# Up projection of a hybrid block: which engine makes the token operands, where the raw rows lie, and weights that stay across the change of tokens

## The chip, the cores and the metric

One core of one Trainium2 chip runs the whole kernel. The metric is device time in microseconds (us), median of several runs of the same program. TensorE does the matrix products (PE, with its weight loads as PEld), VectorE (DVE) and GpSimd (POOL) do elementwise work, ScalarE (ACT) casts, copies and activations, and the queue of SyncE (SP) issues nearly all transfers.

## The reference, cut to what matters

```python
h = h + concat([y_s5, y_rwkv]) @ w_out          # output projection
hn = rms_norm(h, norm_ffn_g)
h = h + square(relu(hn @ w_up)) @ w_down        # up projection, down projection
return rms_norm(h, norm_final_g)
# 2048 tokens, D_MODEL 1024, D_FF 4096, all float32
```

The change touches only the up projection, `square(relu(hn @ w_up))`.

## The kernel before, in words

**The product.** Every float32 operand is split in a high and a low part: ScalarE casts the high part (`hi`, tiles whose names end in h), and an elementwise subtraction makes the low part (`lo`, names in l). A product is then three matmuls (hh, hl, lh) for each block of 128 of the contraction (`product`, L1322). On top of that the up projection is done as a Strassen-like scheme with seven products in place of eight, in the order `ORDER = (1, 5, 6, 2, 7, 3, 4)` (L1283). The weights of a product are sums of quarter blocks a, b, c, d (`left_sums`, L1286, four additions), and so are the tokens (`right_sums`, L1305, four additions for each half, so eight for a set).

**The loops.** `mlp_up` (L1359) has two halves of the tokens (`hb` 0 and 1, 1024 tokens each). For each half it walks over 16 pairs of output blocks (`f` = 0, 2, ... 30), seven products each, twelve matmuls of 128x128x512 for a product. The token operands `x[n]` (seven of them, 128x1024 twice for `hi` and `lo`) stay for a whole half; the weights of a pair are made anew for each `f` and each half, by the generator `ws()`, which `Ahead` keeps up to `UA` = 4 operands in front.

**The making of token operands.** `xs(hb)` loads six raw rows `xraw` of 4 KB per partition from `x2_dram` (quarters a, b, d, two tiles each) into a ring `raw` of seven buffers (L1372), which it shares with the raw weights `wraw` (two tiles for a pair). The quarter c goes into two buffers of the ring `xrow2` (three buffers, L1398). For each n, `xs` takes the sums (L1309 to L1318), casts (L1402) and subtracts (L1403). In half 0 the sums are on VectorE and four of the fourteen subtractions (n = 2 and 3) on GpSimd; in half 1 the sums are on GpSimd and all subtractions on VectorE. The operands 1, 5, 6 have tiles of their own (`mux`); 2, 7, 3, 4 lie in the tiles of the output projection's weights `wo`, so they can't be written before that projection has ended.

**The change of tokens.** While pair f = 30 of half 0 runs, `xs(1)` writes each operand anew as soon as its last product of half 0 has been issued (L1517 to L1520).

**What comes out.** Four of the seven results of a pair are split again (`operands`, L1464: sum, cast L1468, subtraction L1469) and both parts are written to `hs_d` (L1471). Their tiles come from the ring `ys` (sixteen buffers of 2 KB), which also holds the weights' `hi` and `lo`.

**Before and after.** The output projection (`out_proj`) ends in two calls of `proj` that `mlp_up` makes itself (`last[0]`, `last[1]`), between the first operands. Its pools of the GLU (`oe0`, `oe`) and of the group norm (`opl`) are given back before `mlp_up` opens its own, so the new tiles lie at their addresses: `mux` (48 KB) first, then `mur`, the raw rows (28 KB). `mlp_down` follows.

**Order.** The order of instructions on each queue is not written by hand: a planner takes, at each moment of its own timeline, what is ready and has a buffer, and of several the one that stands first in the program. A load with nothing to wait for can thus be issued far ahead of its place.

Of the kernel before, what the change touches and what calls it, by code (L numbers as in the profile page):

```python
# [7 lines left out]
F32 = mybir.dt.float32  # L8
F32R = mybir.dt.float32r
I32 = mybir.dt.int32  # L10
AF = mybir.ActivationFunctionType
ALU = mybir.AluOpType
AX = mybir.AxisListType
PSUM = bass.MemoryType.PSUM
DRAM = bass.MemoryType.DRAM
P = 128
# [6 lines left out]
def pool_of(tc, **k):  # L23
    return tc.tile_pool(reuse_waits="tile", **k)
# [339 lines left out]
BT = 512  # L364
# [712 lines left out]
UA, DW, DH = 4, 2, 3  # L1077
# [208 lines left out]
def left_sums(eng, q, new):  # L1286

    (a, b), (c, d) = q
    yield a
    s = new()  # L1290
    eng.tensor_tensor(out=s, in0=c, in1=d, op=ALU.add)
    yield s
    s2 = new()
    eng.tensor_tensor(out=s2, in0=s, in1=a, op=ALU.subtract)  # L1294
    yield s2
    yield b
    eng.tensor_tensor(out=c, in0=a, in1=c, op=ALU.subtract)
    yield c
    s = new()
    eng.tensor_tensor(out=s, in0=b, in1=s2, op=ALU.subtract)  # L1300
    yield s
    yield d


def right_sums(eng, q):  # L1305

    (a, b), (_, d) = q
    yield a
    eng.tensor_tensor(out=a, in0=b, in1=a, op=ALU.subtract)  # L1309
    yield a  # L1310
    eng.tensor_tensor(out=a, in0=d, in1=a, op=ALU.subtract)  # L1311
    yield a
    c = q[1][0]
    yield c
    eng.tensor_tensor(out=b, in0=d, in1=b, op=ALU.subtract)  # L1315
    yield b
    yield d
    eng.tensor_tensor(out=a, in0=c, in1=a, op=ALU.subtract)  # L1318
    yield a
# [39 lines left out]
def mlp_up(K, opened, h_dram, x2_dram, norm_g, w_up, hs_dram, hr_dram):  # L1359
# [3 lines left out]
    v, act, g = nc.vector, nc.scalar, nc.gpsimd  # L1363
    H = KT // 2
    from contextlib import ExitStack
    with ExitStack() as st:
        pool_ = lambda **k: st.enter_context(pool_of(tc, **k))
        oc, oy, ops, last = opened
        xp, rp, cp, hp, psp = pool_(name="mux", bufs=1), pool_(name="mur", bufs=1), pool_(name="muc", bufs=1), pool_(name="muh", bufs=1), pool_(name="mups", bufs=2, space=PSUM)
        gain = column(K, cp, norm_g[0], KT, "gain2")  # L1370
        wu = w_up[0].rearrange("(k p) m -> p k m", p=P)
        raw = lambda shape, name: rp.tile(shape, F32, tag="raw", bufs=7, name=name)  # L1372
# [10 lines left out]
        def xs(hb):  # L1383

            qs = [[[None, None], [None, None]] for _ in range(0, H, 2)]

            def load(i, j, t, o):
                qs[i][j][t] = o
                nc.sync.dma_start(out=o, in_=x2_dram[hb * 2 + t, :, j * H + 2 * i:j * H + 2 * i + 2])

            for j, t in ((0, 0), (0, 1), (1, 1)):
                for i in range(H // 2):
                    load(i, j, t, raw([P, 2, BT], "xraw"))
            parts = [right_sums((v, g)[hb], q) for q in qs]
            for n in ORDER:
                if n == 2:
                    for i in range(H // 2):
                        load(i, 1, 0, oy.tile([P, 2, BT], F32, tag="xrow2", bufs=3, name="xraw"))  # L1398
                hi, lo = xtile(n)
                for i, part in enumerate(parts):  # L1400
                    r = next(part)
                    act.copy(out=hi[i], in_=r)  # L1402
                    (g if hb == 0 and n in (2, 3) else v).tensor_tensor(out=lo[i], in0=r, in1=hi[i].bitcast(F32), op=ALU.subtract)  # L1403
                hi, lo = ([t[i // 2][:, i % 2] for i in range(H)] for t in (hi, lo))
                x[n] = hi, lo
                yield

        def ws():

            def load(f):  # L1410
                r = [raw([P, H, 2 * P], "wraw") for _ in range(2)]
                for j in range(2):
                    nc.sync.dma_start(out=r[j], in_=wu[:, j * H:j * H + H, f * P:f * P + 2 * P])
                return [[r[j][:, :, i * P:i * P + P] for j in range(2)] for i in range(2)]

            nxt = load(0)
            for n in range(32):
                q = nxt
                for i, o in enumerate(left_sums(g, q, lambda: cp.tile([P, H, P], F32, tag="s", bufs=2, name="ws"))):
                    if i == 0 and n < 31:  # L1420
                        nxt = load(2 * (n + 1) % 32)
                    hi, lo = (oy.tile([P, H, P], F32R, tag="ys", bufs=16, name="w" + s) for s in "hl")
                    act.copy(out=hi, in_=o)  # L1423
                    v.tensor_tensor(out=lo, in0=o, in1=hi.bitcast(F32), op=ALU.subtract)  # L1424
                    yield tuple([t[:, k] for k in range(H)] for t in (hi, lo))

        def last_norm(b):
# [9 lines left out]
            for k in range(KT):  # L1437
# [9 lines left out]
                if k % 2:  # L1447
                    yield

        w, nx = Ahead(ws(), UA), xs(0)  # L1450
        next(nx)
        last[0]()
        w.fill()
        next(nx)
        next(nx)
        last[1]()
        ct = 0

        def hid(name):
            nonlocal ct  # L1460
# [3 lines left out]
        def operands(hb, fp, q):  # L1464

            def split_(n, o):
                hi, lo = (oy.tile([P, BT], F32R, tag="ys", bufs=16, name="h" + s) for s in "hl")
                act.copy(out=hi, in_=o)  # L1468
                v.tensor_tensor(out=lo, in0=o, in1=hi.bitcast(F32), op=ALU.subtract)  # L1469
                for i, t in enumerate((hi, lo)):  # L1470
                    nc.sync.dma_start(out=hs_dram[hb, SPLIT.index(n), fp, i], in_=t.bitcast(F32))  # L1471

            a, c, d = q[1], q[3], q[4]
            s = hp.tile([P, BT], F32, tag="s", bufs=2, name="hs")
            v.tensor_tensor(out=s, in0=c, in1=d, op=ALU.add)
            split_(5, s)
            yield
            v.tensor_tensor(out=c, in0=a, in1=c, op=ALU.subtract)
            split_(7, c)
            yield  # L1480
            v.tensor_tensor(out=s, in0=s, in1=a, op=ALU.subtract)
            split_(6, s)
            yield
            s3 = hp.tile([P, BT], F32, tag="s", bufs=2, name="hs3")
            v.tensor_tensor(out=s3, in0=q[2], in1=s, op=ALU.subtract)  # L1485
            split_(3, s3)

        pend = iter(())
        for hb in range(2):
            for f in range(0, 32, 2):  # L1490
                q = {}

                def finish(o, name, src=None):
                    act.activation(out=o, in_=o if src is None else src, func=AF.Relu)  # L1494
                    act.activation(out=o, in_=o, func=AF.Square)
                    q[name] = o
                    if name in PLAIN:
                        nc.sync.dma_start(out=hr_dram[hb, f // 2, PLAIN.index(name)], in_=o)

                def copy(ps, name):  # L1500
                    o = hid(name)
                    act.copy(out=o, in_=ps)
                    return o

                A, X = (psp.tile([P, BT], F32, tag=n, bufs=2, name="ps_u" + n) for n in "ax")
                B = ops.tile([P, BT], F32, tag="o", bufs=2, name="ps_ub")
                for n in ORDER:
                    lw = w.take()
                    if n not in x:
                        next(nx)  # L1510
                    ps, start = {1: (A, True), 5: (X, True), 6: (A, False), 2: (B, True), 7: (A, False), 3: (X, False), 4: (A, False)}[n]
                    product(K, ps, lw, x[n], start)
                    if f in (2, 4) and hb == 0:
                        if n == 1:
                            ln = last_norm(NT // 256 - 3 + f // 2)
                        next(ln, None)
                    if f == 30 and hb == 0:  # L1517
                        if n == 1:
                            nx = xs(1)
                        next(nx)  # L1520
                    if n == 1:
                        c1 = copy(A, "c1")
                    elif n == 5:
                        c5 = copy(X, "c5")
                    elif n == 6:
                        c2 = copy(A, "c2")
                    elif n == 2:
                        v.tensor_tensor(out=c1, in0=c1, in1=B, op=ALU.add)
                        finish(c1, 1)
                    elif n == 7:  # L1530
                        v.tensor_tensor(out=c5, in0=c5, in1=A, op=ALU.add)  # L1531
                        finish(c5, 4)
                    elif n == 3:
                        v.tensor_tensor(out=c2, in0=c2, in1=X, op=ALU.add)
                        finish(c2, 3)
                    else:
                        finish(hid("c4"), 2, A)
                        pend = operands(hb, f // 2, q)
                    if n in (4, 1, 5, 6):
                        next(pend, None)  # L1540
# [186 lines left out]
```

## Time and profile before

| | |
|---|---|
| median of 3 runs | 2641.9 us (2638.69 to 2647.39) |
| profiled execution | 2643.06 us, span 2641.3 us |
| mean granted TensorE clock | 0.968 |
| PE busy in the span | 93% |
| VectorE, ScalarE, GpSimd busy | 70%, 49%, 35% |

The profile is of one execution. Times in it are us from the start of the span. "Releaser" (an arrow to the left) is what ended the idle time before an instruction. A busy PE is not a PE at its peak, so the number of matmuls in a stretch says more than its busy time.

### The profile page before, as it was taken

How to read it: one execution, taken by the hardware profiler on the slowest of the kernel's cores; microseconds unless marked ns; L12 is line 12 of the kernel's file. 1: busy time of each engine (PE TensorE's matmuls, PEld its weight loads, DVE VectorE, ACT ScalarE, POOL GpSimd, SP SyncE). 2: the span in 40 equal slices, each digit the busy share in tenths (PEclk: the TensorE clock that was granted, in tenths of full speed). 3: DMA queues.
4: the chain of work that ended last, by engine and by line, in shares of the span. 5: the costliest groups of instructions: out<-in, count | busy, mean ns of one | idle time of the engine just before them, and what ended most of it. 6: DMA issues, size and time to landing. Idle time of an engine off the chain costs nothing. (4 is left out here: it accounts for less than half of the span.)

```text
span 2641.3 us, 38268 instructions
## 1 busy us (share of the span) xinstructions
PE 2459.0 (93%) x13084; PEld 2032.2 (77%) x13084; DVE 1845.4 (70%) x3177; ACT 1301.6 (49%) x2558; POOL 917.0 (35%) x812
## 2 busy tenths in 40 slices
PE   7999989998989888999799997999988999999997
PEld 7987667786889887888588785878866777777775
DVE  7568797579677768665867669766655566655665
ACT  6355545555444456454576665666643233332333
POOL 1058798602222224220423235332212222323333
PEclk9999989999989998999899998999999999999999
DMA  9655738996876554343576664655576455554545
GB/s 290 205 165 172 217 118 252 255 245 173 172 156 153 131 148 162 137 149 122 183 256 213 208 206 160 228 199 196 183 291 230 148 172 167 165 178 149 176 148 182
DMA packets 543187, 492.55 MB, mean 186 GB/s; under 512 B 187312, under 2 KB 445360, under 8 KB 542992
## 3 DMA queue, kind: packets, MB, share of 16 engines
q1 hardware_dynamic: 542704, 489.05, 59.9%
q8 instruction: 104, 1.70, 0.3%
q10 hardware_dynamic: 288, 1.05, 0.1%
q14 instruction: 91, 0.75, 0.1%
HBM read 304.27 MB, written 180.49 MB: 184 GB/s over the span
## 5 line engine op out<-in xcount | busy, mean ns | idle before, releaser
L1606 POOL TENSOR_TENSOR acc<-acc,c 128x512 f32<-128x512 f32 x128 | 192.4, 1524 | 487.5 <-ACT c L1610 463.4
L1610 ACT COPY c<-ps_da 128x512 f32<-128x512 f32 x192 | 106.3, 588 | 267.2 <-PE ps_da L1328 265.8
L433 PE MATMUL ps_z<-xh,wh 128*128 128x512 f32 x448 | 184.5, 412 | 15.3 <-DVE zr L617 5.7
L435 PE MATMUL ps_z<-xh,wl 128*128 128x512 f32 x448 | 181.6, 406 | 0.0
L434 PE MATMUL ps_z<-xl,wh 128*128 128x512 f32 x448 | 181.1, 404 | 0.0
L1606 DVE TENSOR_TENSOR acc<-acc,ps_dx 128x512 f32<-128x512 f32 x128 | 87.6, 685 | 122.4 <-PE ps_dx L1328 119.8
L1424 DVE TENSOR_TENSOR wl<-wraw,wh 128x512 fp32r<-128x512 f32 x128 | 124.3, 972 | 13.3 <-ACT wh L1423 8.7
L1294 POOL TENSOR_TENSOR ws<-ws,wraw 128x512 f32<-128x512 f32 x32 | 53.4, 1667 | 210.0 <-DVE wl L1424 209.8
L374 ACT CAST hh<-hr 128x512 fp32r<-128x512 f32 x96 | 59.6, 621 | 126.5 <-PE ps_da L1328 91.4
L433 PEld LDWEIGHTS ps_z<-xh,wh 128*128 128x128 f32 x448 | 87.6, 195 | 39.9 <-DVE zr L617 7.5
L1494 ACT ACTIVATE c<-c 128x512 f32<-128x512 f32 x96 | 60.5, 632 | 107.1 <-DVE c L1531 56.9
L913 POOL TENSOR_TENSOR DT<-dtc,cst 128x128 f32<-128x128 f32 x128 | 55.8, 466 | 159.1 <-PE ps_pq L920 105.5
L609 DVE TENSOR_TENSOR wl<-wr,wh 128x1024 fp32r<-128x1024 f32 x56 | 86.2, 1539 | 34.4 <-ACT wh L608 34.0
L433 PE MATMUL ps_o<-woh,ys 128*128 128x512 f32 x256 | 103.1, 403 | 1.1 <-ACT woh L1124 0.6
L434 PE MATMUL ps_o<-wol,ys 128*128 128x512 f32 x256 | 102.1, 400 | 0.2 <-DVE wol L1125 0.2
L435 PEld LDWEIGHTS ps_z<-xh,wl 128*128 128x128 f32 x448 | 87.2, 195 | 19.2 <-issue 0.2
L434 PEld LDWEIGHTS ps_z<-xl,wh 128*128 128x128 f32 x448 | 87.4, 195 | 18.8 <-issue 0.9
L435 PE MATMUL ps_o<-woh,ys 128*128 128x512 f32 x256 | 100.6, 396 | 0.0
L1300 POOL TENSOR_TENSOR ws<-wraw,ws 128x512 f32<-128x512 f32 x32 | 45.5, 1422 | 147.6 <-DVE wl L1424 147.6
L1469 DVE TENSOR_TENSOR hl<-hs,hh 128x512 fp32r<-128x512 f32 x96 | 74.4, 775 | 23.4 <-ACT hh L1468 21.4
L1424 DVE TENSOR_TENSOR wl<-ws,wh 128x512 fp32r<-128x512 f32 x96 | 83.9, 880 | 8.6 <-ACT wh L1423 7.4
L1468 ACT CAST hh<-hs 128x512 fp32r<-128x512 f32 x96 | 59.8, 623 | 52.3 <-DVE hs L1485 20.7
(692 smaller groups left out, 8263.3 us busy)
## 6 DMA issues: line engine op xcount, KB each, us to landing
hs<-hs_d SPq DMA_DIRECT2D x128, 512.0 KB
wraw<-in_w_up SPq DMA_DIRECT2D x64, 512.0 KB
hs_d<-hh SPq DMA_DIRECT2D x128, 256.0 KB
hs_d<-hl SPq DMA_DIRECT2D x128, 256.0 KB
wr<-in_w_in SPq DMA_DIRECT2D x56, 512.0 KB
hr_d<-c SPq DMA_DIRECT2D x96, 256.0 KB
hr<-hr_d SPq DMA_DIRECT2D x96, 256.0 KB
xrow<-in_x SPq DMA_DIRECT2D x32, 512.0 KB
```

Source lines behind the costliest of these rows:

```text
L374: nc.scalar.copy(out=hi, in_=raw)
L433: K.nc.tensor.matmul(out, lh, rh, start=i == 0, stop=False)
L434: K.nc.tensor.matmul(out, lh, rl, start=False, stop=False)
L435: K.nc.tensor.matmul(out, ll, rh, start=False, stop=i == n - 1)
L609: v.tensor_tensor(out=wl, in0=wr, in1=wh.bitcast(F32), op=ALU.subtract)
L913: g.tensor_tensor(out=DT[:, p], in0=bc(dtc[:, u, p:p + 1, :], [P, 4, 32]), in1=c["m4"].rearrange("p (a x) -> p a x", a=4), op=ALU.mult)
L1424: v.tensor_tensor(out=lo, in0=o, in1=hi.bitcast(F32), op=ALU.subtract)
L1468: act.copy(out=hi, in_=o)
L1469: v.tensor_tensor(out=lo, in0=o, in1=hi.bitcast(F32), op=ALU.subtract)
L1494: act.activation(out=o, in_=o if src is None else src, func=AF.Relu)
L1606: add = lambda eng, o, s: eng.tensor_tensor(out=o, in0=o, in1=s, op=ALU.add)
L1610: act.copy(out=t, in_=ps)
```

## The change

Six edits in `mlp_up`. The raw rows' pool is opened before that of the token operands 1, 5, 6, so the two trade places. All sums and all subtractions for the token operands are VectorE's, in both halves. The sums for the weights of pairs n = 0, 15 and 16 are VectorE's too (of the others GpSimd's). In half 1 the pair f = 30 comes first and uses the weights that half 0 made for it: these seven operands (14 buffers of `ys`) are kept, and one load and one making of weights is left out (31 in place of 32). The load of the raw weights behind the change of tokens is put after the last sum of pair 15, and in half 1 the raw quarter a is loaded last. The split results (`hh`, `hl`) leave the ring `ys` and take one buffer of `xrow2` (three buffers) for both parts. At the start fewer weights are made ahead, operand 5 is written in the program before `last[0]`, and operands 6 and 2 before `last[1]`.

```diff
-        xp, rp, cp, hp, psp = pool_(name="mux", bufs=1), pool_(name="mur", bufs=1), pool_(name="muc", bufs=1), ...
+        rp, xp, cp, hp, psp = pool_(name="mur", bufs=1), pool_(name="mux", bufs=1), pool_(name="muc", bufs=1), ...
...
-            for j, t in ((0, 0), (0, 1), (1, 1)):
+            for j, t in (((0, 0), (0, 1), (1, 1)), ((0, 1), (1, 1), (0, 0)))[hb]:
                 for i in range(H // 2):
                     load(i, j, t, raw([P, 2, BT], "xraw"))
-            parts = [right_sums((v, g)[hb], q) for q in qs]
+            parts = [right_sums(v, q) for q in qs]
...
-                    (g if hb == 0 and n in (2, 3) else v).tensor_tensor(out=lo[i], in0=r, in1=hi[i].bitcast(F32), op=ALU.subtract)
+                    v.tensor_tensor(out=lo[i], in0=r, in1=hi[i].bitcast(F32), op=ALU.subtract)
...
-            for n in range(32):
+            for n in range(31):
                 q = nxt
-                for i, o in enumerate(left_sums(g, q, lambda: cp.tile([P, H, P], F32, tag="s", bufs=2, name="ws"))):
-                    if i == 0 and n < 31:
+                for i, o in enumerate(left_sums(v if n in (0, 15, 16) else g, q, lambda: cp.tile([P, H, P], F32, tag="s", bufs=2, name="ws"))):
+                    if i == (6 if n == 15 else 0) and n < 30:
                         nxt = load(2 * (n + 1) % 32)
...
-        w, nx = Ahead(ws(), UA), xs(0)
+        w, nx = Ahead(ws(), 0), xs(0)
+        next(nx)
+        w.fill()
         next(nx)
         last[0]()
-        w.fill()
-        next(nx)
-        next(nx)
+        for w.n in (1, 2):
+            w.fill()
+            next(nx)
         last[1]()
-        ct = 0
+        w.n = UA
+        ct, kept = 0, []
...
             def split_(n, o):
-                hi, lo = (oy.tile([P, BT], F32R, tag="ys", bufs=16, name="h" + s) for s in "hl")
+                t = oy.tile([P, 2, BT], F32R, tag="xrow2", bufs=3, name="hh")
+                hi, lo = t[:, 0], t[:, 1]
...
         for hb in range(2):
-            for f in range(0, 32, 2):
+            for f in (range(0, 32, 2), (30, *range(0, 30, 2)))[hb]:
...
                 for n in ORDER:
-                    lw = w.take()
+                    if hb and f == 30:
+                        w.fill()
+                        lw = kept.pop(0)
+                    else:
+                        lw = w.take()
+                        if f == 30:
+                            kept.append(lw)
```

## Rows read from the trace of the kernel before

**Rows 1.** Page, part 1: busy us, share of span, instructions.

```profile
PE 2459.0 (93%) x13084; PEld 2032.2 (77%) x13084; DVE 1845.4 (70%) x3177; ACT 1301.6 (49%) x2558; POOL 917.0 (35%) x812
```

**Rows 2.** Stretches, products' line L1328: length, PE (x matmuls), PEld, clock, DMA share, GB/s.

```profile
1272.00:1295.00 23.00, 7.98 (x19) 5.47 (x20) 0.66 0.46 143
1400.00:1580.00 180.00, 179.07 (x772) 144.29 (x772) 1.00 0.61 205
1597.00:1650.00 53.00, 38.19 (x141) 28.31 (x142) 0.87 0.56 184
```

**Rows 3.** Timeline of PE at the start: start, us, [idle before and releaser].

```profile
1279.16 0.80 PE L1328 MATMUL ps_ua<-x1h,wl 128*128 128x512 f32 x1 [6.17 <-DVE wl L1424]
1288.55 0.80 PE L1328 MATMUL ps_ux<-x5h,wh 128*128 128x512 f32 x1 [5.25 <-ACT wh L1423]
```

**Rows 4.** VectorE's groups, 1258 to 1307: count, busy, mean ns, idle before.

```profile
L1424 DVE TENSOR_TENSOR wl<-wraw,wh 128x512 fp32r<-128x512 f32 x6 | 9.9, 1678 | 0.5 <-ACT wh L1423 0.5
L1311 DVE TENSOR_TENSOR xraw<-xraw 128x1024 f32<-128x1024 f32 x2 | 5.7, 2825 | 0.0
...
L1309 DVE TENSOR_TENSOR xraw<-xraw 128x1024 f32<-128x1024 f32 x2 | 2.4, 1218 | 0.0
```

**Rows 5.** Timeline of SP's queue at the start: loads of tokens and weights.

```profile
1251.94 5.80 SPq L1389 DMA_DIRECT2D xraw<-x_d  x7
...
1268.60 0.32 SPq L1389 DMA_DIRECT2D xraw<-x_d  x1
1276.43 10.88 SPq L1413 DMA_DIRECT2D wraw<-in_w_up  x4
1291.39 1.51 SPq L1389 DMA_DIRECT2D xraw<-x_d  x2
```

**Rows 6.** Timeline of VectorE, 1246 to 1292: ends of GLU and group norm, last sums.

```profile
1246.02 1.43 DVE L1115 TENSOR_TENSOR ys<-sig,ys 128x256 fp32r<-128x256 f32 x4
...
1255.85 0.43 DVE L1115 TENSOR_TENSOR ys<-b,ys 128x256 fp32r<-128x256 f32 x1 [0.47 <-ACT ys L1114]
...
1290.15 2.35 DVE L1318 TENSOR_TENSOR xraw<-xraw 128x1024 f32<-128x1024 f32 x2
```

**Rows 7.** Timeline of PE at the change of tokens.

```profile
1634.18 0.79 PE L1328 MATMUL ps_ux<-x3h,wl 128*128 128x512 f32 x1 [3.91 <-DVE wl L1424]
```

**Rows 8.** VectorE's groups at the change of tokens, 1588 to 1651.

```profile
L1424 DVE TENSOR_TENSOR wl<-wraw,wh 128x512 fp32r<-128x512 f32 x8 | 11.4, 1424 | 0.0
L1469 DVE TENSOR_TENSOR hl<-hs,hh 128x512 fp32r<-128x512 f32 x6 | 9.6, 1602 | 0.0
...
L1478 DVE TENSOR_TENSOR c<-c,c 128x512 f32<-128x512 f32 x2 | 1.4, 685 | 0.0
```

**Rows 9.** The same stretch, line L1403 alone: length, DVE (x instructions), POOL.

```profile
1588.00:1651.00 63.00, 24.85 (x14) 0.00 (x0) 0.89 0.51 167
```

**Rows 10.** GpSimd's groups at the change of tokens: costliest of four like it.

```profile
L1315 POOL TENSOR_TENSOR xraw<-xraw 128x1024 f32<-128x1024 f32 x2 | 6.2, 3090 | 0.0
```

**Rows 11.** Timelines of VectorE and GpSimd, one overlap at 1621.

```profile
1621.62 3.44 DVE L1403 TENSOR_TENSOR x7l<-xraw,x7h 128x1024 fp32r<-128x1024 f32 x1
1621.18 2.79 POOL L1318 TENSOR_TENSOR xraw<-xraw 128x1024 f32<-128x1024 f32 x1 [2.49 <-DVE x6l L1403]
```

**Rows 12.** SP's queue: first and last of the six raw rows for half 1.

```profile
1557.97 0.61 SPq L1389 DMA_DIRECT2D xraw<-x_d  x1
...
1617.01 0.32 SPq L1389 DMA_DIRECT2D xraw<-x_d  x1
```

**Rows 13.** Page, part 5: subtraction and cast of the split results.

```profile
L1469 DVE TENSOR_TENSOR hl<-hs,hh 128x512 fp32r<-128x512 f32 x96 | 74.4, 775 | 23.4 <-ACT hh L1468 21.4
...
L1468 ACT CAST hh<-hs 128x512 fp32r<-128x512 f32 x96 | 59.8, 623 | 52.3 <-DVE hs L1485 20.7
```

**Rows 14.** One write of a split result: SP's issue, then DMA share and GB/s behind it.

```profile
1591.55 0.32 SPq L1471 DMA_DIRECT2D hs_d<-hh  x1
1593.30:1594.10 0.80, 0.80 (x5) 0.67 (x4) 0.80 (x1) 0.00 (x0) 0.00 (x0) 1.00 0.00 0
```

More of the change, by code (lines that the diff above doesn't have):

```diff
@@ L1368, in mlp_up @@
         oc, oy, ops, last = opened
-        xp, rp, cp, hp, psp = pool_(name="mux", bufs=1), pool_(name="mur", bufs=1), pool_(name="muc", bufs=1), pool_(name="muh", bufs=1), pool_(name="mups", bufs=2, space=PSUM)
+        rp, xp, cp, hp, psp = pool_(name="mur", bufs=1), pool_(name="mux", bufs=1), pool_(name="muc", bufs=1), pool_(name="muh", bufs=1), pool_(name="mups", bufs=2, space=PSUM)
         gain = column(K, cp, norm_g[0], KT, "gain2")
```

## The prediction

> **What bounds the kernel now.** I read the page first: TensorE is busy 93% of the span, the other engines far less [rows 1]. So I looked for the places in which TensorE does fewer matmuls than it can, in stretches of the up projection's line. In the steady part, 1400 to 1580, it does 772 matmuls in 180 us, 0.233 us each [rows 2]. A pair of output blocks is 84 of them, 19.6 us. At the start, 1272 to 1295, there are 19 matmuls, worth 4.4 us, in 23 us: 18.6 us lost. At the change of tokens, 1597 to 1650, there are 141, worth 32.9 us, in 53 us: 20.1 us lost [rows 2]. The granted clock is 0.66 and 0.87 of full in these two stretches, where the steady one has 1.00; what that costs is within the two losses, as matmuls are counted. Together 38.7 us are at stake in this stage, and the change touches little else.
>
> Next, who ends the waits. At the start TensorE waits 6.17 us for the low part of the first weights (VectorE) and 5.25 us for the cast of the second ones [rows 3]; at the change of tokens 3.91 us again for a low part of weights [rows 7]. These are short operations, so I looked at what stood ahead of them on VectorE. Two 128x1024 sums at the start took 1.218 us each and two others of the same form 2.825 us; 128x512 subtractions that need 0.685 us took 1.678 us on the mean [rows 4, 8]. At the change of tokens the fourteen subtractions for tokens took 24.85 us [rows 9], which at 1.218 would be 17.1, and eight subtractions of weights 11.4 where 5.5 would do [rows 8]. VectorE is stretched there, not only busy. A pair of rows shows by what: a VectorE operation of 3.44 us starts 0.4 us behind a GpSimd operation of 2.79 us [rows 11]: 2.4 us waiting and then its own 1.2, less the overlap of neighbours. GpSimd itself takes up to 3.09 us for a sum that VectorE makes in 1.218 [rows 4, 10].
>
> The Trainium skill, page "SBUF — State Buffer", section "Who interferes with whom", says that a VectorE instruction with two inputs in SBUF and a GpSimd one that reads SBUF exclude each other for a whole instruction, by order of issue; the overlap agrees (3.44 us). Its page "Perfetto Trace Analysis", section "Optimizing Scalar/DVE Operations", speaks against this change: with VectorE saturated, handing work to ScalarE or GpSimd may make sense. By that rule alone the sum below would end at 2663; it is the second rival.
>
> **The change, part by part.**
>
> *Sums and subtractions to VectorE, at the start.* Four subtractions of 128x1024 come from GpSimd (4 x 1.218 = 4.9 us) and four weight sums of 128x512 (4 x 0.685 = 2.7): 7.6 us more work. What goes is the stretching: six subtractions of weights 9.9 - 4.1 = 5.8, two sums 5.7 - 2.4 = 3.3 [rows 4], and as much again in the subtractions for operands 5, 6 and 7 by the same measure (my estimate 4 to 5). About 14 less, 7.6 more: some 6 us shorter. Bounds: all of it stays (7.6 longer), or the waits were all GpSimd's (14 shorter); I take 6, as the overlapping rows are nearest.
>
> *Raw rows where the GLU's buffers lay.* Seven token loads go out over 5.8 us from 1251.94 [rows 5], paced by tiles of the group norm, whose last use ends at 1256.3, while the GLU's last use ends at 1247.5 [rows 6]. With places traded the loads can start some 4 us earlier, and operands 1, 5 and 6 can be made ahead of the crowd. Operands 2, 7, 3, 4 still wait for the output projection's weights, until near 1272, where the up projection's stretch begins [rows 2]. One wait stays: seven raw buffers hold six token rows and one weight row, and the second weight row is issued only when a token row falls free, now 1276.43 [rows 5]. Operand 7 or 3 must have been made for that; I put this at about 1272, so the weights of product 5 at about 1279, where it now starts at 1288.55 [rows 3]. The loss at the start goes from 18.6 to about 5 (product 1 ends near 1275, a wait of 3 to 4 us, and a little of clock): 13 to 14 us won. Bounds: 2 (only the wait for the row counts, and comes 2 us earlier) to 18.6.
>
> *Operands earlier in the program.* Loads of c now come ahead of the output projection's last two rows in the shared ring `xrow2`. The last row waits for the row before it, not for c; I cost this at nothing, the cover being the two PSUM banks that still hold the sums. Without cover it is one 128x512 addition and a load, 3 to 5 us.
>
> *Sums to VectorE at the change of tokens.* Eight sums of 128x1024 come from GpSimd, 8 x 1.218 = 9.7 us, and the weight sums of pairs 15 and 16, 8 x 0.685 = 5.5. The kept weights take away seven subtractions, 4.8, and seven casts on ScalarE. Gone is the stretching: 24.85 - 17.1 = 7.8 [rows 9], 11.4 - 5.5 = 5.9 and 9.6 - 4.1 = 5.5 [rows 8], and some 3 in smaller groups: 22 us. Net about 12 us off a VectorE that is busy without a gap for 63 us there.
>
> *Order of loads.* The last of the six raw rows for half 1 is issued at 1617.01, in the middle of the stalls; the six are spread over 59 us, 12 us apart on the mean, as weights for the next pair hold two of seven buffers [rows 12]. With the weight load behind them the tokens get these two, so the sixth goes out two places earlier, near 1593. And the kept pair is 19.6 us in which no new weights are needed.
>
> Together the loss at the change goes from 20.1 to about 6: 14 us won. Counted: a product is 12 x 0.233 = 2.8 us, and from the end of pair 30's first one it is twelve products, 33.6 us, until operand 4 is needed; the token work is 22 operations of 1.218 = 26.8, with some 11 us of results and weights in between (16 operations of 0.685); about 4 us too many, and I allow 2 for the first weights behind the change. Bounds: 0 (loads still late) to 20.
>
> *Split results in `xrow2`.* Here is a hidden cost. The two c rows for half 1 were loaded at 1291.39, 1.2 us after the start of the two sums that gave their buffers free and 290 us ahead of use [rows 5, 6]. Eight loads belong to half 0, so these two are half 1's: the planner loads them as soon as a buffer is there. It will do so again, and then two of the three buffers are taken for all of half 0, and the split results go through the one left. One passage: cast 0.62, subtraction 0.78 [rows 13], and a write that has left the queues 1.75 us after its issue (1591.55, nothing moving from 1593.30) [rows 14]: 3.2 us, with a queue of one VectorE operation 3.9. Four in a pair: 13 to 16 us, under the pair's 19.6. So it is covered by the products, and I charge 3 us over half 0 for casts that block ScalarE's queue (weights and PSUM copies stand behind them). If cover is gone it is a rival.
>
> *Left out.* One load of weights, 4 sums on GpSimd, 14 operations: hidden work, nothing beyond the above. The start of the down projection is costed at nothing; its weights' buffers come free a little earlier or later, bounds -3 to +3.
>
> **The sum**, against the profiled execution's 2643.1 us: -13.5 - 14 + 3 = -24.5, so 2618.6. Its span is 1.8 us less than its own time, and the median of the runs, 2641.9, lies 1.2 below it; on the median's scale 2617.5. I say 2618.
>
> **The rivals.**
>
> *Only half comes.* The stalls are bound by loads, not by VectorE: the second weight row still waits, or the last token row. Then one place gives 13 and the other nothing: about 2631. For it: the 1276.43 load; against it: the releasers are VectorE's and ScalarE's.
>
> *VectorE is the bound whoever does the sums.* If its long operations are long for another cause, it gets 7.6 more at the start and 9.7 + 5.5 - 4.8 = 10.4 more at the change: +18 and 3, so 2663. Against it: the two durations of one form in one stretch [rows 4].
>
> *The ring of one, slower than before.* If a passage takes 5.5 us (a subtraction behind two others, a write in a full DMA), four take 22.0 us, 2.4 more than a pair; over 15 pairs 36 us. With 27.5 won: 2643 - 27.5 + 36 = 2652. It decides from 4.9 us a passage on, and turns the sign at 5.35. For it: the hoisted c rows; against it: 3.2 to 3.9 counted.
>
> *Nothing moves.* The planner makes another order with stalls as long: 2636 to 2646.
>
> **How the numbers follow.** Chances: forecast (2604 to 2630) 0.60, only half 0.16, nothing moves 0.10, ring of one 0.08, VectorE the bound 0.06. All 38.7 us won would be 2604, the low end. To hold 8 in 10 the range takes in the half case and most of "nothing": 2604 to 2643; the forecast's own is 2606 to 2630. No change that a measurement can tell is within 0.3%, 8 us, 2634 to 2650. Faster: 0.60 + 0.14 = 0.74; same: 0.10 + 0.02 + 0.02 = 0.14; slower: 0.12.
>
> **What would show it.** Right: 128x1024 operations of VectorE at 1.2 us throughout and none on GpSimd at either place; product 5 starting before 1281; the last raw row for half 1 issued before the last product of half 0; under 30 matmuls' worth lost at each place. The c rows loaded soon after the start, with casts of results some 4 us apart, would show the ring of one; steady pairs above 19.6 us in half 0 alone would show that it costs. Wrong: equal stretching without GpSimd, or TensorE waiting for `xraw` loads.

## The result, and the profile after

| | before | after |
|---|---|---|
| median of the runs (four each) | 2640.3 us | 2613.09 us (2607.68 to 2615.8) |
| profiled execution, span | 2641.3 us | 2614.0 us |
| ratio after to before, 95% interval | | 0.9886 (0.9862 to 0.991) |

The forecast was 2618 us, 2604 to 2643, faster with a chance of 0.74. The time is 27 us lower, by the interval 24 to 36. The sum had 24.5 us. But the two places gave other parts of it than predicted, and that is what this section and the experiments are about.

The spans can't be set against each other directly. Between the start and the last row of the GLU both kernels run the same instructions, and yet that row starts at 1246.02 before [rows 6] and at 1240.31 after. A second profile of the changed kernel, taken later, has it at 1245.39, and over all the profiles of this study it lies between 1240.31 and 1253.56: it is the spread of executions. So I measure the stage by itself, from that row on VectorE to the first product of the down projection on TensorE. Of the kernel before, the timeline of TensorE:

```profile
1953.12 0.80 PE L1328 MATMUL ps_da<-w0h,hh 128*128 128x512 f32 x1 [9.80 <-ACT hh L374]
```

And after, the timelines of VectorE and of TensorE:

```profile
1240.31 1.43 DVE L1115 TENSOR_TENSOR ys<-sig,ys 128x256 fp32r<-128x256 f32 x4
...
1921.25 0.79 PE L1328 MATMUL ps_da<-w0h,hh 128*128 128x512 f32 x1 [8.81 <-ACT hh L374]
```

Before, the stage takes 1953.12 - 1246.02 = 707.1 us; after, 1921.25 - 1240.31 = 680.9, which is 26.2 less. In the second profile of the changed kernel it is 1925.87 - 1245.39 = 680.5:

```profile
1245.39 1.43 DVE L1115 TENSOR_TENSOR ys<-sig,ys 128x256 fp32r<-128x256 f32 x4
...
1925.87 0.79 PE L1328 MATMUL ps_da<-w0h,hh 128*128 128x512 f32 x1 [7.97 <-ACT hh L374]
```

The two executions agree within half a microsecond, where their spans (2614.0 and 2611.4) differ by 2.6. No other kernel has two profiles, so how far one stage can be off is known from this pair alone.

**The change of tokens.** Stretch 1580 to 1680 of the products' line, first before, then after (length, PE busy, matmuls, clock, DMA share, GB/s):

```profile
1580.00:1680.00 100.00, 85.12 (x344) 0.93 0.58 193
```

```profile
1400.00:1580.00 180.00, 180.00 (x778) 1.00 0.58 198
1580.00:1680.00 100.00, 100.00 (x433) 1.00 0.68 231
```

After, TensorE has no gap there: 433 matmuls where before had 344. The 89 more are 20.6 us at 180 / 778 = 0.231 us each, which is the whole of the loss [rows 2]. VectorE's groups at the change, 1588 to 1651, and line L1404 alone (x subtractions, busy) in the same stretch:

```profile
L1425 DVE TENSOR_TENSOR wl<-wraw,wh 128x512 fp32r<-128x512 f32 x10 | 7.9, 792 | 0.2 <-ACT wh L1424 0.2
...
L1483 DVE TENSOR_TENSOR c<-c,c 128x512 f32<-128x512 f32 x3 | 3.1, 1046 | 0.0
```

```profile
1588.00:1651.00 63.00, 12.03 (x10) 1.00 0.73 250
```

The ten subtractions for tokens take 1.20 us each, where the fourteen of before took 1.78 [rows 9]. The stretching is gone from these, less so from the small ones: GpSimd still makes weight sums behind pair 16, and 0.68 us become 0.79 and 1.05. The tokens also start earlier. SP's queue, the eight loads for half 1:

```profile
1518.85 0.32 SPq L1389 DMA_DIRECT2D xraw<-x_d  x1
1531.80 7.14 SPq L1389 DMA_DIRECT2D xraw<-x_d  x2
...
1570.62 0.32 SPq L1389 DMA_DIRECT2D xraw<-x_d  x1
1593.24 0.32 SPq L1389 DMA_DIRECT2D xraw<-x_d  x1
1598.47 0.32 SPq L1389 DMA_DIRECT2D xraw<-x_d  x1
```

The last two are the c rows: ScalarE's cast for operand 2, which is the first to need one, waits for a load at 1597.74. So the last raw row goes out at 1570.62, where before it was 1617.01 [rows 12], and the c rows are loaded here and not 290 us ahead, as they were [rows 5].

**The start.** TensorE's timeline, the waits between 1250 and 1300:

```profile
1256.33 0.50 PE L1328 MATMUL ps_ua<-x1h,wh 128*128 128x512 f32 x1 [1.42 <-ACT wh L1424]
...
1262.19 0.62 PE L433 MATMUL ps_o<-woh,ys 128*128 128x512 f32 x1 [2.54 <-DVE xrow L1225]
...
1282.44 0.79 PE L1328 MATMUL ps_ux<-x5h,wh 128*128 128x512 f32 x1 [7.35 <-ACT wh L1424]
```

Product 1 now runs inside the output projection, but that projection gets a wait of its own, 2.54 us for an addition on VectorE, and product 5 starts 1282.44 - 1240.31 = 42.1 us behind the GLU's last row; before it was 1288.55 - 1246.02 = 42.5 [rows 3, 6]. Only behind product 5 is something won: matmuls follow each other at 0.23 us from 1286.4, 46 us behind that row, before from 1296.2, 50 us behind it. Stretch 1240 to 1400, all of TensorE's work, first before, then after:

```profile
1240.00:1400.00 160.00, 144.79 (x632) 0.95 0.63 214
```

```profile
1240.00:1400.00 160.00, 148.69 (x645) 0.97 0.64 220
```

TensorE is idle 11.3 us there, before 15.2 (and as long in the 155 us behind the GLU's last row of each): the start gave 4 us. SP's queue and VectorE say what product 5 waited for:

```profile
1244.76 0.50 SPq L1414 DMA_DIRECT2D wraw<-in_w_up  x1
...
1274.89 5.51 SPq L1414 DMA_DIRECT2D wraw<-in_w_up  x5
```

```profile
1251.09 2.36 DVE L1404 TENSOR_TENSOR x1l<-xraw,x1h 128x1024 fp32r<-128x1024 f32 x2 [0.53 <-ACT x1h L1403]
...
1273.64 2.35 DVE L1404 TENSOR_TENSOR x7l<-xraw,x7h 128x1024 fp32r<-128x1024 f32 x2
...
1281.05 0.68 DVE L1291 TENSOR_TENSOR ws<-wraw 128x512 f32<-128x512 f32 x1
```

The second weight row goes out at 1274.89, as the first half of operand 7's subtraction (1273.64 and 1.2 us) gives a raw buffer free; its sum starts at 1281.05. From the GLU's last row that issue is 34.6 us away, before 30.4 [rows 5]: 4 us later, though the token rows were loaded earlier (1241.79, with the GLU's end).

**Behind the stage** the down projection took 2614.0 - 1921.25 = 692.8 us in this execution, 685.5 in the second profile, 688.2 before. So the 27.3 us between the spans are 5.7 that came ahead of the stage, 26.2 in it and 4.6 lost behind it, of which the first and the last are spread.

### The profile page after: what moved, and what is told of

It is laid out like the page before. It is cut to its first block, busy times and chain, and to the rows that moved or that the text cites. A ratio compares the mean times of both kernels' runs of the same rounds, so it can differ in the third digit from the quotient of the medians.

```text
span 2614.0 us, 38287 instructions
## 1 busy us (share of the span) xinstructions
PE 2447.6 (94%) x13084; PEld 2026.7 (78%) x13084; DVE 1844.5 (71%) x3194; ACT 1301.2 (50%) x2551; POOL 851.4 (33%) x784
## 3 DMA queue, kind: packets, MB, share of 16 engines
q10 hardware_dynamic: 288, 1.05, 0.1%
## 4 chain that ended last, share of the span: by engine, by line
PE 65%; DVE 13%; DMA 12%; issue 3%; ACT 3%; POOL 2%; SPq 2%; POOLq 0%; DVEq 0%; ACTq 0%
PE ps_ua L1328 13%; PE ps_da L1328 9%; PE ps_ux L1328 7%; PE ps_dx L1328 4%; PE ps_ub L1328 3%; PE ps_db L1328 2%; DMA wraw<-in_w_down 2%; PE ps_o L433 2%; PE ps_o L434 2%; PE ps_o L435 2%; PE ps_z L433 1%; PE ps_z L434 1%; PE ps_z L435 1%; DMA wr<-in_w_in 1%; DVE wl L609 1%
## 5 line engine op out<-in xcount | busy, mean ns | idle before, releaser
L1425 DVE TENSOR_TENSOR wl<-wraw,wh 128x512 fp32r<-128x512 f32 x124 | 103.8, 838 | 29.5 <-ACT wh L1424 29.2
L1291 POOL TENSOR_TENSOR ws<-wraw 128x512 f32<-128x512 f32 x28 | 41.2, 1471 | 202.1 <-DMA hs_d<-hh 72.8
L1424 ACT CAST wh<-wraw 128x512 fp32r<-128x512 f32 x124 | 76.1, 616 | 54.0 <-PE ps_ua L1328 34.9
L1425 DVE TENSOR_TENSOR wl<-ws,wh 128x512 fp32r<-128x512 f32 x93 | 66.8, 721 | 29.5 <-ACT wh L1424 25.0
L1474 DVE TENSOR_TENSOR hh<-hs,hh 128x512 fp32r<-128x512 f32 x96 | 79.7, 830 | 10.5 <-ACT hh L1473 9.7
```

## The experiments

The theory to test: VectorE's long operations on two inputs wait out whole GpSimd operations, and that is what TensorE waited for at the change of tokens. Its rivals: the kept pair and the order of loads did it; and at the start, the places of the raw rows or the program's order did what was won. Each run is told with its ratio to the kernel before and with the length of the stage as measured above (707.1 before, 680.9 and 680.5 after).

### All of GpSimd's work back

```diff
-parts = [right_sums(v, q) for q in qs]
+parts = [right_sums((v, g)[hb], q) for q in qs]
-v.tensor_tensor(out=lo[i], ...)
+(g if hb == 0 and n in (2, 3) else v).tensor_tensor(out=lo[i], ...)
-left_sums(v if n in (0, 15, 16) else g, ...)
+left_sums(g, ...)
```

> The changed kernel with GpSimd back in its old work (the sums for tokens of half 1, the subtractions of operands 2 and 7 at the start, the weight sums of pairs 0, 15 and 16), while kept weights, order of loads, places and program order stay as changed. If GpSimd's overlap with VectorE was what cost the time, most of the 20.7 us that came at the change of tokens go again: 2623 to 2633 us, with 128x1024 operations of VectorE at 1.6 us and more on the mean between 1550 and 1660. If the kept pair and the order of loads carry the gain, it stays within 4 us of the changed kernel, 2609 to 2617, and TensorE stays without a gap at the change although VectorE is stretched.

At the start the subtractions that go back are those of operands 2 and 3 (`n in (2, 3)`), not 2 and 7 as the expectation has it.

Measured: 2641.72 us, ratio 0.9984 (0.9964 to 1.0005), stage 700.1. More went than the theory said: by the times next to nothing of the change is left, by the stage 7.0 us. The 128x1024 operations of VectorE take 1.71 us on the mean between 1550 and 1660, as expected. Stretch 1580 to 1680 and TensorE's longest wait in it:

```profile
1580.00:1680.00 100.00, 88.48 (x359) 0.95 0.57 192
```

```profile
1598.27 0.79 PE L1328 MATMUL ps_ux<-x5l,wh 128*128 128x512 f32 x1 [6.09 <-DVE x5l L1404]
```

74 of the 89 matmuls are lost again (17.1 us), although the kept pair, the order of loads and the places are as changed and the first loads for half 1 go out at 1524.95 and 1537.90, about as early as in the changed kernel. The wait shown, for tokens, is 6.1 of the 11.5 us in which TensorE is idle; 2.9 are waits for weights and 2.6 for results that have to leave PSUM.

### VectorE's sums alone, on the kernel before

The same three lines, the other way, in the kernel before.

> The kernel before with VectorE alone making the sums (the same operations moved as in the change) and nothing else changed. Stretching theory: VectorE loses its waits for GpSimd at both places; the late last raw row stays, so 8 to 15 us come, 2625 to 2632. If kept pair and loads carry the gain, VectorE has 15 us more work in the same 63 us at the change and all eight weight products behind it: 2637 to 2650.

Measured: 2630.15 us, ratio 0.9935 (0.9917 to 0.9954), stage 693.5. As the theory said: 13.6 us of the stage's 26.2. Stretch 1580 to 1680:

```profile
1580.00:1680.00 100.00, 90.68 (x371) 0.95 0.62 202
```

### The kept pair undone, and the kept pair alone

```diff
-for n in range(31):
+for n in range(32):
...
-if i == (6 if n == 15 else 0) and n < 30:
+if i == 0 and n < 31:
...
-for f in (range(0, 32, 2), (30, *range(0, 30, 2)))[hb]:
+for f in range(0, 32, 2):
```

and `lw = w.take()` for every pair; then the same edit, the other way, in the kernel before.

> The changed kernel with 32 pairs of weights made again, in the old order of pairs and with the weight load at the head of its pair; VectorE alone for the sums, order of token loads, places and program order stay as changed. Stretching theory: VectorE has 4.8 us more work and the weights stand between the tokens; 3 to 8 us go, 2616 to 2621. If the kept pair carries the gain, 12 to 20 us go, 2625 to 2633, with waits of TensorE for the low part of weights behind pair 30 of half 0.

> The kernel before with only the kept weights and the later weight load of pair 15; GpSimd keeps its sums, order of token loads as before. Stretching theory: 5 us or less come, 2635 to 2642, and VectorE's subtractions at the change of tokens stay at 1.7 us on the mean. If the kept pair carries the gain, 12 to 20 us come, 2620 to 2628, and the stretched operations cost TensorE nothing.

Measured: undone 2628.63 us, ratio 0.9939 (0.9918 to 0.9959), stage 689.5, 387 matmuls; alone 2643.7 us, ratio 0.9998 (0.9982 to 1.0014), stage 703.5, 361 matmuls. Both runs also move the load of the raw weights behind the change, so what they say of the kept pair holds for the two together. Alone it is worth nothing that the times tell, and 3.6 us by the stage, as the stretching theory had it. Undone, it costs 8.6 us of the stage, and by the ratios 0.9939 - 0.9886 = 0.0053, 14 us, give or take 8; the theory had 3 to 8, the rival 12 to 20, and which is nearer stays open. What TensorE waits for without it:

```profile
1616.43 0.79 PE L1328 MATMUL ps_ux<-x5h,wh 128*128 128x512 f32 x1 [4.55 <-ACT wh L1424]
```

This is a wait for the first new weights, not for tokens. With the kept pair alone it is the other way round: stretch 1580 to 1680 of that run, and TensorE's longest waits in it (us in total, times, longest):

```profile
1580.00:1680.00 100.00, 87.26 (x361) 0.98 0.58 194
```

```profile
PE ps_ua L1328 <- ACT c L1502: 4.7, 3, 1.6
PE ps_ux L1328 <- DVE x5l L1403: 3.3, 1, 3.3
PE ps_ua L1328 <- DVE x6l L1403: 2.1, 1, 2.1
PE ps_ua L1328 <- ACT c L1494: 1.7, 1, 1.7
```

The waits for weights are gone (7.9 us in the kernel before), those for tokens stay (5.4, before 6.4), and 7.2 us of waits for copies of results out of PSUM are new (before 0.5). In this run the split results still come from the ring `ys`, of which the kept weights hold fourteen of sixteen buffers; in the changed kernel they don't. Whether the new waits come from that was not tried, so the run doesn't show what the kept pair would be worth alone with buffers enough.

So more than one wait stands in this place, and they cover each other: with GpSimd's sums the tokens are late, though the weights are not; with VectorE's sums the weights are late, unless a pair needs none. One edit removes 27 of the 89 matmuls' loss, the other 17, all edits together 89. By the stages, VectorE's sums give 13.6 us, the kept pair on top of everything else 8.6, and what is left between them is 4.0 us and 16 matmuls (371 to 387). That is the order of the token loads or the new ring of the split results, as the places and the program order of the start lose no matmul at the change when undone (433 in both runs below); neither of the two was tried by itself.

### Which of GpSimd's operations

```diff
-parts = [right_sums(v, q) for q in qs]
+parts = [right_sums((v, g)[hb], q) for q in qs]
```

and, in another kernel, `left_sums(g, ...)` for all pairs, with the tokens left to VectorE.

> The changed kernel with only the eight 128x1024 sums for tokens of half 1 back on GpSimd. If it is the length of GpSimd's operations on two inputs that VectorE waits out (2.6 to 3.3 us each), this alone brings back most of what all of GpSimd's old work brought back at the change of tokens (74 matmuls' worth, 17 us): 10 to 17 us slower than the changed kernel, a ratio to before of 0.992 to 0.996. If it was the sum of many small overlaps, half of it: 0.990 to 0.991.

> The changed kernel with only the weight sums of pairs 0, 15 and 16 back on GpSimd (128x512, about 1.4 us each). By the length of the operations 0 to 5 us go, and TensorE loses less than 5 us at the change of tokens: a ratio of 0.988 to 0.990. If the small sums matter as much as the long ones, 8 us and more: above 0.9915.

Measured: tokens 2635.22 us, ratio 0.9954 (0.9938 to 0.9969), stage 697.1, 362 matmuls; weights 2621.11 us, ratio 0.9905 (0.9886 to 0.9924), stage 685.4, 419 matmuls. The changed kernel, beside them on the same chip, stood at 2617.43 (0.9888). The first lies in the range that was expected for the length of the operations; the second is just above its own and can't be told from the changed kernel. The eight long sums alone bring back 71 of the 74 matmuls that all of GpSimd's work lost at the change; the short ones 14, some 3 us, and 4.5 to 4.9 of the whole stage. Two timelines of the first, GpSimd and VectorE from 1588 on, show how:

```profile
1588.77 2.39 POOL L1309 TENSOR_TENSOR xraw<-xraw 128x1024 f32<-128x1024 f32 x1 [30.24 <-DVE x1l L1404]
1591.24 2.73 POOL L1315 TENSOR_TENSOR xraw<-xraw 128x1024 f32<-128x1024 f32 x1
1595.14 2.78 POOL L1309 TENSOR_TENSOR xraw<-xraw 128x1024 f32<-128x1024 f32 x1 [1.17 <-DVE x1l L1404]
```

```profile
1589.60 0.69 DVE L1543 TENSOR_TENSOR c<-c,ps_ua 128x512 f32<-128x512 f32 x1 [0.96 <-PE ps_ua L1328]
1590.20 1.51 DVE L1425 TENSOR_TENSOR wl<-wraw,wh 128x512 fp32r<-128x512 f32 x1
1591.93 3.13 DVE L1404 TENSOR_TENSOR x1l<-xraw,x1h 128x1024 fp32r<-128x1024 f32 x1 [0.21 <-ACT x1h L1403]
...
1595.59 3.41 DVE L1404 TENSOR_TENSOR x5l<-xraw,x5h 128x1024 fp32r<-128x1024 f32 x1
```

The subtraction at 1591.93 finds GpSimd's sum under way until 1591.24 + 2.73 = 1593.97 and ends at 1595.06, 1.1 us behind that. The next one, at 1595.59, ends at 1599.00, 1.1 us behind the end of GpSimd's third sum (1597.92). The operands are also a chain through both engines: the eight sums on GpSimd take 2.4 to 3.3 us in place of 1.2, and the two subtractions shown 1.9 and 2.2 us more than alone. How much of the 17 us is the slower sum and how much VectorE's waiting, these runs don't separate.

### The start: places, program order, a buffer for the eighth row

```diff
-rp, xp, cp, hp, psp = pool_(name="mur", bufs=1), pool_(name="mux", bufs=1), ...
+xp, rp, cp, hp, psp = pool_(name="mux", bufs=1), pool_(name="mur", bufs=1), ...
```

> The changed kernel with the raw rows and the operands at their old places. If the places give the start its gain (the loads go out some 4 us earlier by them), 3 to 5 us go: 2616 to 2618 us, with the first six token loads out near the end of the group norm again. If product 5 is bound by the second weight row alone, which waits for a token row anyway, the time stays at 2610 to 2616.

```diff
-w, nx = Ahead(ws(), 0), xs(0)
+w, nx = Ahead(ws(), UA), xs(0)
 next(nx)
-w.fill()
-next(nx)
 last[0]()
-for w.n in (1, 2):
-    w.fill()
-    next(nx)
+w.fill()
+next(nx)
+next(nx)
 last[1]()
```

> The changed kernel with the old program order at the start (operand 1 ahead of the last two pieces of the output projection, 5 and 6 between them, 2 behind both, four weights made ahead at once). If the earlier operands are worth the start's gain, 3 to 6 us go, 2616 to 2619. If what they bring is eaten by the new wait of the output projection (2.54 us, for an addition on VectorE) and its late rows, the time stays at 2610 to 2616 and that wait is gone.

```diff
-for w.n in (1, 2):
-    w.fill()
-    next(nx)
-last[1]()
+w.n = 1
+w.fill()
+next(nx)
+last[1]()
+w.n = 2
+w.fill()
+next(nx)
```

> The changed kernel with one step moved: operand 2 (and with it the two c rows) behind the last piece of the output projection, operands 1, 5 and 6 stay ahead. If the c rows in the shared ring keep the output projection's last rows late, its wait of 2.54 us goes and 2 to 4 us come: 2609 to 2611. If VectorE's order or the second weight row is the bound at the start, the time stays within 2 us of 2613 or operand 2 is late and 2 to 4 us go.

```diff
-load(i, j, t, raw([P, 2, BT], "xraw"))
+load(i, j, t, hp.tile([P, 2, BT], F32, tag="s", bufs=1, name="xraw") if hb == 0 and (i, j, t) == (1, 1, 1) else raw([P, 2, BT], "xraw"))
...
-s = hp.tile([P, BT], F32, tag="s", bufs=2, name="hs")
+ss = hp.tile([P, 2, BT], F32, tag="s", bufs=1, name="hs")
+s, s3 = ss[:, 0], ss[:, 1]
...
-s3 = hp.tile([P, BT], F32, tag="s", bufs=2, name="hs3")
```

> The changed kernel with a place of its own for the last token row of half 0 (in the buffers of the result sums, which are not used before the first pair ends; later both result sums share one tile there), so that the second weight row has a raw buffer at once. If product 5 waits for that row (7.35 us, for the cast of its weights), 4 to 7 us come: 2606 to 2609, with the row out before 1250. If VectorE's queue is the bound at the start, product 5 starts within 2 us of 1282 all the same and the time stays at 2610 to 2616.

The last two together, beside the changed kernel once more:

> The changed kernel with both earlier edits: the eighth token row in the result sums' buffers, and operand 2 with its c rows behind the last piece of the output projection. By the stretch from the GLU's last row to the first product of the down projection each alone took 3 to 5 us off. If they add, 5 to 8 us under the changed kernel in the same call: a ratio 0.002 to 0.003 lower. If both touch the same wait, or if VectorE's order at the start is the bound, it equals it within 0.001.

> The changed kernel once more, unaltered, to stand beside the other three on the same chip, and for a second profile: the GLU's last row, whose instructions and those ahead of it are the same as before, is expected at 1244 to 1250 and not at 1240.31 again if that was the spread of executions; the change of tokens without a gap again, product 5 waiting some 7 us again. Ratio 0.987 to 0.991.

| | median, us | ratio to before | stage, us | TensorE idle in 1240 to 1400, us |
|---|---|---|---|---|
| changed kernel | 2613.09 | 0.9886 (0.9862 to 0.991) | 680.9 | 11.3 |
| changed, again | 2617.43 | 0.9888 (0.9868 to 0.9908) | 680.5 | 11.1 |
| old places | 2618.12 | 0.9892 (0.9871 to 0.9913) | 683.5 | 12.7 |
| old start | 2620.68 | 0.9916 (0.9888 to 0.9943) | 677.8 | 11.4 |
| operand 2 behind | 2618.41 | 0.9891 (0.987 to 0.9911) | 678.3 | 10.8 |
| eighth row | 2612.62 | 0.9878 (0.9859 to 0.9898) | 676.2 | 5.2 |
| eighth row, operand 2 behind | 2615.71 | 0.9879 (0.986 to 0.9898) | 674.9 | 5.8 |

The medians are of several chips; each ratio is to the kernel before on the same one. No ratio here can be told from the changed kernel's: the intervals overlap. By the stage's length, of one execution each, the old places cost 2.5 us and the eighth row gives 4.8 (4 to 7 had been expected of the times); operand 2 behind gives 2.6, as does the old order (3.2), although the old order has the highest ratio. So the new program order brought nothing that these runs show; whether it costs or gives a few us stays open. Eighth row and operand 2 together are 6.0 us shorter by the stage, but by the ratio only 0.0009 lower, where 0.002 to 0.003 had been expected if they add.

What gave the start its 4 us, two earlier runs show. Stretch 1240 to 1400 of TensorE, first with VectorE's sums alone on the kernel before, then with all of GpSimd's work back in the changed kernel:

```profile
1240.00:1400.00 160.00, 148.57 (x647) 0.97 0.67 225
```

```profile
1240.00:1400.00 160.00, 144.90 (x636) 0.97 0.64 218
```

TensorE is idle 11.4 us in the first and 15.1 in the second, where the changed kernel has 11.3 and the kernel before 15.2. All of the 4 us come with the work that went from GpSimd to VectorE; places and program order together add nothing to it.

The eighth row shows what product 5 waited for. SP's queue, then TensorE, of that kernel:

```profile
1254.31 1.00 SPq L1414 DMA_DIRECT2D wraw<-in_w_up  x2
```

```profile
1269.02 0.40 PE L1328 MATMUL ps_ux<-x5h,wh 128*128 128x512 f32 x1
1270.67 0.51 PE L1328 MATMUL ps_ux<-x5l,wh 128*128 128x512 f32 x1 [1.26 <-DVE x5l L1404]
1272.48 0.79 PE L1328 MATMUL ps_ux<-x5h,wl 128*128 128x512 f32 x1 [1.30 <-DVE wl L1425]
```

Both weight rows go out together, product 5 starts 1269.02 - 1249.81 = 19.2 us behind the GLU's last row in place of 42.1, its wait of 7.35 us is gone, and TensorE is idle 6.1 us less. What held product 5 was thus a missing buffer, which VectorE gave free only with operand 7. It is the best candidate of the study by the trace, and not shown faster by the times.

## Why the prediction was right, and where it was not

**What bounds it.** Right: the losses at the two places, and the cause read from two durations of one form in one stretch [rows 4] and from one overlap [rows 11]. With the long sums back on GpSimd, subtractions take 3.1 and 3.4 us, of which 1.1 lie behind the end of GpSimd's sum, and the change of tokens is late again. How much of that is the wait of the subtractions and how much the slower sums stays open.

**Sums at the change, order of loads, kept pair: -14 forecast, about -20.6 measured.** The mechanism was right and the term mis-sized. I left 6 us over: 4 for VectorE being that much too slow for the last operand, 2 for the first weights behind the change. Neither is there. In the trace operand 1's subtraction starts at 1574.43 and the last one of operand 4 at 1615.30, 42 us to its end for the 22 operations, where the count had 38, and TensorE waits for none of them. What the count had wrong is the time at hand, twelve products or 33.6 us. Operand 1's last product of half 0 ends, and operand 4's first one of half 1 starts, here:

```profile
1577.12 0.39 PE L1328 MATMUL ps_ua<-x1h,wl 128*128 128x512 f32 x1
...
1621.91 0.39 PE L1328 MATMUL ps_ua<-x4h,wh 128*128 128x512 f32 x1
```

That is 44.6 us, sixteen products: the planner puts products of the neighbouring pairs between. The raw rows were also all issued by 1570.62, and I had put the sixth near 1593. The kept pair I had booked as 4.8 us of VectorE's time; without it product 5 waits 4.55 us for the new weights.

**The start: -13.5 forecast, about -4 measured.** The mis-sized term is the second weight row. The step "operand 7 or 3 must have been made for that" held: it is operand 7's subtraction that frees the buffer. The date I gave it, 1272, did not; on the clock of the execution before, 1274.89 is 1280.6. I took VectorE's 6 us of saving for an earlier operand 7, but from 1251.09 VectorE works through operands 1, 5, 6 and 2 with hardly a gap, 1.2 us an operation, and operand 7 comes last but two. That is the mechanism of the rival "only half comes" (the second weight row still waits), at one place, though the time is not that rival's, as the other place gave more than all of its share.

**Operands earlier, costed at nothing.** Wrong by 2.5 us and more: the output projection waits 2.54 us for a row's addition. The c rows, issued at 1214.08 and 1233.12, took two of the ring's three buffers, and the projection's last two rows were issued only at 1256.86 and 1265.53. I named the cover, the two PSUM banks; it was too short. Behind the wait TensorE also works at its lower clock, 1.2 GHz: nine matmuls 0.43 us apart in place of 0.23, with a granted clock (third figure from the end) of 0.53, where it was 1.00 in the 4 us before 1262.

```profile
1262.20:1265.60 3.40, 3.40 (x9) 0.53 0.39 154
```

Moving operand 2 alone behind removes this wait. Product 5 then waits 8.86 us in place of 7.35, so TensorE is idle only 0.5 us less in all, but the stage is 2.6 us shorter.

**Split results in `xrow2`, +3 forecast, none seen.** The step that failed is "it will do so again": the c rows of half 1 were not loaded at the start but at 1593.24 and 1598.47. Before, no other use of that ring stood between the two sets of c rows; now the split results of half 0 do, and the loads behind them in the program came behind them on the queue. (That the split results kept them back is read from the order; it was not tried by itself.) So there was no ring of one, and 778 matmuls in 1400 to 1580, where before had 772, show no cost. What a ring of one would have cost was not tried.

**Sum.** -4 and -20.6 and 0 make -24.6; the stage itself measures -26.2 (the steady stretch has six matmuls more, 1.4 us), the medians -27.2. The forecast's -24.5 came out of errors that cancel: 9.5 too much at the start, 6.6 and 3 too little elsewhere. That the sum came so near was luck; that the time fell, and at which places it could, was not. The rival "VectorE the bound whoever does the sums" (2663) fell, and with it the rule of the Trainium skill that was weighed for it: page "Perfetto Trace Analysis", section "Optimizing Scalar/DVE Operations". The same section adds that moving work between GpSimd and VectorE may not help, as they share a read port; here moving it off GpSimd, with nothing else changed, gave 0.9935.

**The signs named ahead.** Right: no 128x1024 operation on GpSimd at either place, and 1.2 us for each of them; the last raw row ahead of half 0's last product; no matmul lost at the change. Wrong: product 5 before 1281 (1282.44, in an execution that ran 5.7 us ahead; 1287.36 in the second), and fewer than 30 matmuls' worth lost at the start (11.3 us idle are 49).

## What to carry to other kernels

Where two engines make one chain of operands, look at the durations of one form of instruction in one stretch: if they fall into two groups, the longer ones hold somebody else's time, and the helper can be worth less than nothing although both engines look busy. Two waits at one place hide each other, so undo edits one at a time from the new kernel as well as adding them one at a time to the old: the kept pair was worth nothing by the times alone (3.6 us by the stage) and 9 to 14 us with the rest. An edit tried alone can also meet a bound that the rest of the change has removed, as the kept weights may have done in the ring `ys`. And cost an earlier load by the release of its buffer, counted through all the work that stands ahead of that release on its engine, not by how much that engine saves in total.

## What the runs showed of the hardware

A GpSimd operation holds up a VectorE one that reads two operands in SBUF, but not one that reads PSUM: at 1589.60, in the middle of GpSimd's sum (1588.77 to 1591.16), the addition with `ps_ua` took its 0.69 us, and the subtraction behind it, at 1590.20, took 1.51 in place of 0.68 and ended 0.55 us behind that sum. The Trainium skill, page "SBUF — State Buffer", section "Who interferes with whom", says so: at most one input in SBUF doesn't contend, two do. The trace agrees. It holds beyond this place: in the stage of the kernel before, 34 operations of 128x512 with an operand in PSUM start in the midst of a GpSimd sum or subtraction, and all take 0.67 to 0.69 us, as the others do; eleven 128x1024 operations with both operands in SBUF start so and take 1.69 to 3.44 us, and the other 21 take 1.21 to 1.23. (Spans of GpSimd in a profile are rough.)

With the same instructions ahead of it, the GLU's last row came between 1240.31 and 1253.56 in the profiles of this study, which is half of the whole gain; the length of the stage between two fixed instructions repeated within 0.5 us in the one kernel profiled twice.
